# Gathering the hidden rows of 64 dense tokens during the routing, and plain float32 operands for the U blocks done ahead

## The chip, the cores and the metric

The kernel runs on one core of one Trainium2 chip. Its engines are TensorE (PE, with its weight loads as PEld), VectorE (DVE), ScalarE (ACT), GpSimd (POOL) and SyncE (SP), which here only issues transfers. The metric is the device time of one execution in microseconds, as the median of the runs.

## The reference, cut to what matters

One encoder layer for 512 tokens of width 1024: two attentions, a layer norm, and then

```
h = LN2(alpha * h + PEER(h) + sigmoid(h @ W_g + b_g) * (p @ W_ple))
```

PEER is a feed-forward layer with 16384 single-neuron experts, row e of U and of V being expert e. For each token and each of 8 heads, the query's two halves are scored against 128 sub-keys each, the 16 best of each half are combined, and the 16 best sums give 16 experts e = 128 * e1 + e2 with softmax weights g. So 128 experts for a token:

```
PEER(h)[t] = sum over its 128 experts e of  g[t, e] * gelu(U[e] . h[t]) * V[e]
```

## The kernel before, in words

The attentions and the first layer norm leave h (four tiles of 128 tokens, h[0] to h[3]) and its transpose in two parts, hTh and hTl, in a reduced float32 format (fp32r), whose sum is h. A product of two such pairs is three matmuls (mm3, L89 to L92: high by high, high by low, low by high); split (L72) makes the parts, a cast on ScalarE (L75) and a subtraction on VectorE (L76). stream (L81) loads a block as raw and splits it into whi and wlo.

PEER is computed in two ways. The first 128 tokens (chunk 0, N_G) are *gathered*: for each of their 128 experts k, gather_u (L861) fetches one row of U per token by an indirect transfer that POOL issues (128 rows of 4 KB into a gat buffer, of which there are four), and VectorE forms the 128 dot products with h (L865). After all 128, one Gelu and one multiplication by the weights; then gather_v does the same with V and adds into base (L876). That is 257 steps. The other 384 tokens (chunks 1 to 3, N_D) are *dense*: all 16384 experts are computed in 128 blocks of 128. expert_in (L616) loads a U block, splits it, and makes its hidden values for all 384 tokens, 24 matmuls of 128x384 into hp, then Gelu (L623) into ge. expert_out (L886) multiplies the activations a = ge * G, split into a_hi and a_lo, by the V block, 18 matmuls of 128x512 into six acc tiles that stay in PSUM. G holds the weights of all tokens for all experts, zero where an expert isn't chosen.

G is made in the routing. route (L691) finds for a chunk the expert numbers (as e1 and e2) and weights gw, on VectorE; for chunk 0 it ends in i_sel (L760), the list for the gathers. build_g (L764) turns e1, e2 and gw of a dense chunk into rows of G: per token a one-hot matrix by e1 and a weighted one by e2 (L779 to L788), one plain float32 matmul (L793), a copy on ScalarE (L796), and a store (L797) to g_dram. Since this leaves TensorE idle, a generator filler (L803) yields other work: the output gate (8 steps with its products, L821 to L824), and the first LEAD = 40 U blocks, of which the first SPILL = 16 go to ge_dram and the others stay in ge buffers. run_fill takes 1.6 filler steps per step of route and 0.9 per step of build_g. The chunks are routed in the order 1, 2, 3, 0. In this part a scheduler orders each engine's instructions.

The main loop (L905 to L947) goes over the 128 blocks. VectorE's order is as written there. Each step n does expert_in(n + 40) while there is one, loads every eighth step a gt tile with G for eight blocks (load_g, L897 to L902), loads the V block as v_raw (L914) and splits it, multiplies ge by gt (L932), splits the result, does expert_out, and then as many gather steps as are due: 257 / (128 - 0.75 * LEAD - 3) for a step with an expert_in, a quarter of that for one without. The pools of the routing (pR: rt, rg) are closed ahead of it, and pE, with gt, gat, v_raw, v_hi, v_lo, a_hi and a_lo, takes their memory. whi, wlo and raw come from wst, which stays.

At the end (L958) acc is added to base, and the last layer norm and the stores follow.

Of the kernel before, what the change touches and what calls it, by code (L numbers as in the profile page):

```python
# [9 lines left out]
F32 = mybir.dt.float32  # L10
F32R = mybir.dt.float32r
I32 = mybir.dt.int32
# [7 lines left out]
T = 512  # L20
# [7 lines left out]
QD = 96  # L28
N_G = 128
N_D = T - N_G  # L30
GT = 16
GB = 8
LEAD = 40
SPILL = 16
FILL_ROUTE = 1.6
FILL_G = 0.9
OT = 8
OV = 5
NEG = -1e30
# [12 lines left out]
def tile_encoder_layer(ctx: ExitStack, tc: tile.TileContext, A: dict, out: bass.AP):  # L52
# [16 lines left out]
    def r32(ap):  # L69
        return ap.bitcast(F32)  # L70
# [10 lines left out]
    def stream(src, shape, scale=None):  # L81
        raw = wst.tile([128] + shape, F32, name="raw", bufs=3)
        nc.sync.dma_start(raw, src)
        hi = wst.tile([128] + shape, F32R, name="whi")
        lo = wst.tile([128] + shape, F32R, name="wlo")
        split(hi, lo, raw, scale)
        return hi, lo
# [514 lines left out]

    NGC, NDC = N_G // 128, N_D // 128
    NTG = N_D // GT
    ts = slice(N_G, T)
    u_rows, v_rows = A["u_rows"], A["v_rows"]
    ge_dram = dram.tile([SPILL, 128, N_D], F32, name="ge_dram")
    g_dram = dram.tile([NTG, 128, 128 * GT], F32, name="g_dram")

    pB = ctx.enter_context(tc.tile_pool(name="pB", bufs=1))  # L610
# [2 lines left out]
    i_sel = pB.tile([128, NGC, 128], I32, name="i_sel")  # L613
    ge_t = {}

    def expert_in(i):  # L616

        u = stream(A["uT"][i], [8, 128])
        ps = psH.tile([128, 512], F32, name="hp")
        for k in range(8):  # L620
            mm3(ps[:, :N_D], (u[0][:, k], u[1][:, k]), (hTh[:, k, ts], hTl[:, k, ts]), k == 0, k == 7)
        ge = pB.tile([128, N_D], F32, name="ge", bufs=LEAD - SPILL + 2)
        nc.scalar.activation(ge, ps[:, :N_D], AF.Gelu)  # L623
        if i < SPILL:
            nc.sync.dma_start(ge_dram[i], ge)
        else:
            ge_t[i] = ge
# [63 lines left out]
    def route(c, res):  # L691

        v = v_all[:, c]
        ixf = rt.tile([128, 8, 2, 16], F32, name="tk_if")
        nc.vector.tensor_copy(ixf, i_all[:, c])
        cand = rt.tile([128, 8, N_CAND], F32, name="cand")

        def v1(a, na, n):
            return v[:, :, 0, a:a + na].unsqueeze(3).to_broadcast([128, 8, na, n])

        def v2(na, n):
            return v[:, :, 1, 0:n].unsqueeze(2).to_broadcast([128, 8, na, n])

        a = 0
        while a < 16:
            na = sum(1 for x in ROW_N if x == ROW_N[a])
            n = ROW_N[a]
            o = cand[:, :, ROW_ST[a]:ROW_ST[a] + na * n].rearrange("p h (a n) -> p h a n", n=n)
            nc.vector.tensor_tensor(o, v1(a, na, n), v2(na, n), op=OP.add)
            a += na  # L710
        cv = rt.tile([128, 8, 16], F32, name="cv")
        ci = rt.tile([128, 8, 16], U32, name="ci")
        for hd in range(8):
            tmp = rt.tile([128, N_CAND], F32, name="tk_t2", bufs=2)
            top16(cv[:, hd], ci[:, hd], cand[:, hd, :], tmp)
        yield
        cif = rt.tile([128, 8, 16], F32, name="cif")
        nc.vector.tensor_copy(cif, ci)
        gw = g_sel[:, c, :] if c < NGC else rt.tile([128, 128], F32, name="gw")
        g3 = gw.rearrange("p (h k) -> p h k", k=16)  # L720
        nc.vector.tensor_tensor(g3, cv, cv[:, :, 0:1].to_broadcast([128, 8, 16]), op=OP.subtract)
        nc.scalar.activation(gw, gw, AF.Exp)
        wt = rt.tile([128, 8, 16], F32, name="wt")
        nc.vector.tensor_copy(wt[:, :, 0:1], ixf[:, :, 0, 0:1])
        nc.vector.tensor_tensor(wt[:, :, 1:16], ixf[:, :, 0, 1:16], ixf[:, :, 0, 0:15], op=OP.subtract)
        nc.vector.scalar_tensor_tensor(wt, wt, 64.0, dst_c.unsqueeze(1).to_broadcast([128, 8, 16]),
                                       op0=OP.mult, op1=OP.add)
        big = rt.tile([128, 8, 16, 16], F32, name="big")
        b3 = big.rearrange("p h k a -> p (h k) a")
        cf = cif.rearrange("p h k -> p (h k)")  # L730
        nc.vector.tensor_tensor(b3, cf.unsqueeze(2).to_broadcast([128, 128, 16]),
                                start_c.unsqueeze(1).to_broadcast([128, 128, 16]), op=OP.is_ge)
        yield
        gs = rt.tile([128, 8], F32, name="gs")
        nc.vector.reduce_sum(gs, g3, axis=AX.X)
        nc.vector.reciprocal(gs, gs)
        nc.vector.tensor_tensor(g3, g3, gs.unsqueeze(2).to_broadcast([128, 8, 16]), op=OP.mult)
        nc.vector.tensor_tensor(big, big, wt.unsqueeze(2).to_broadcast([128, 8, 16, 16]), op=OP.mult)
        es = rt.tile([128, 128], F32, name="es")
        nc.vector.reduce_sum(es, b3, axis=AX.X)  # L740
        ei = rt.tile([128, 128], I32, name="ei")
        nc.vector.tensor_copy(ei, es)
        sti = rt.tile([128, 128], I32, name="sti")
        nc.vector.tensor_scalar(sti, ei, 63, None, op0=OP.bitwise_and)
        nc.vector.tensor_scalar(ei, ei, 6, None, op0=OP.arith_shift_right)
        e1 = rt.tile([128, 128], F32, name="e1")
        nc.vector.tensor_copy(e1, ei)
        bb = rt.tile([128, 128], F32, name="bb")
        nc.vector.tensor_copy(bb, sti)
        nc.vector.tensor_tensor(bb, cf, bb, op=OP.subtract)  # L750
        yield
        big = rt.tile([128, 8, 16, 16], F32, name="big")
        b3 = big.rearrange("p h k a -> p (h k) a")
        nc.vector.tensor_tensor(b3, bb.unsqueeze(2).to_broadcast([128, 128, 16]),
                                iota[:, 0:16].unsqueeze(1).to_broadcast([128, 128, 16]), op=OP.is_equal)
        nc.vector.tensor_tensor(big, big, ixf[:, :, 1, :].unsqueeze(2).to_broadcast([128, 8, 16, 16]), op=OP.mult)
        e2 = rt.tile([128, 128], F32, name="e2")
        nc.vector.reduce_sum(e2, b3, axis=AX.X)
        if c < NGC:
            nc.vector.scalar_tensor_tensor(i_sel[:, c, :], e1, 128.0, e2, op0=OP.mult, op1=OP.add)  # L760
        res.extend((e1, e2, gw))
        yield
# [35 lines left out]
            yield  # L798


    gb = row_bcast(rg, A["gate_b"], "gb")

    def filler():  # L803
        blocks = iter(range(LEAD))
        for hf in range(2):
            hs = slice(hf * 512, (hf + 1) * 512)
            gps = [ps_tile("mm", 4) for _ in range(4)]
            for kk in range(4):
                w = stream(A["gate_w"][kk * 256:(kk + 1) * 256, hs].rearrange("(k p) n -> p k n", p=128), [2, 512])
                for k2 in range(2):  # L810
                    k = 2 * kk + k2
                    for c in range(4):
                        cs = slice(c * 128, (c + 1) * 128)
                        mm3(gps[c], (hTh[:, k, cs], hTl[:, k, cs]), (w[0][:, k2], w[1][:, k2]), k == 0, k == 7)
                yield

            for c in range(4):
                pl = rg.tile([128, 512], F32, name="pl", bufs=2)
                nc.sync.dma_start(pl, ple_dram[c, :, hs])
                z = rg.tile([128, 512], F32, name="z", bufs=2)  # L820
                nc.vector.tensor_tensor(z, gps[c], gb[:, hs], op=OP.add)  # L821
                nc.scalar.activation(z, z, AF.Tanh, scale=0.5)
                nc.vector.scalar_tensor_tensor(z, z, 1.0, pl, op0=OP.add, op1=OP.mult)
                nc.vector.scalar_tensor_tensor(base[c][:, hs], h[c][:, hs], ALPHA, z, op0=OP.mult, op1=OP.add)  # L824
                if c % 2:
                    expert_in(next(blocks))
                    yield
        for i in blocks:
            expert_in(i)
            yield  # L830

    fill = filler()
# [7 lines left out]
            due -= 1  # L840

    run_fill(0)
    for c in list(range(NGC, 4)) + list(range(NGC)):
        res = []
        for _ in route(c, res):
            run_fill(FILL_ROUTE)
        if c >= NGC:
            for _ in build_g(c, *res):
                run_fill(FILL_G)
    for _ in fill:  # L850
        pass
    pR.close()
# [52 lines left out]
    with tc.manual_schedule(engines={nc.vector.engine}):  # L905
        for n, i in enumerate(order):
# [17 lines left out]
                al = pE.tile([128, N_D], F32R, name="a_lo")  # L924
            split(vh, vl, raw)
            if i < SPILL:
                ge = pE.tile([128, N_D], F32, name="ge_in", bufs=2)
                nc.sync.dma_start(ge, ge_dram[i])
            else:
                ge = ge_t.pop(i)  # L930
            g3 = ge.rearrange("p (g t) -> p g t", t=GT)
            nc.vector.tensor_tensor(g3, g3, gt[:, :, n % GB, :], op=OP.mult)  # L932
            split(ah, al, ge)
            late.append((n, ah, al, vh, vl))
            if n < 124:
                for c in range(NDC):
# [112 lines left out]
```

## Time and profile before

| | |
|---|---|
| time, median of 3 runs (lowest to highest) | 1650.75 us (1648.87 to 1651.54) |
| the profiled execution's own time | 1650.28 us |
| its span | 1648.4 us |
| granted TensorE clock, mean | 0.994 |
| q1, transfers issued by SP and others | 234.52 MB, 41.3% of 16 engines' span |
| q0, indirect transfers issued by POOL | 140.00 MB, 24.2% |
| read from HBM, written | 339.61 MB, 32.51 MB |
| landing of a U block, a V block, a gt tile (median) | 6.2, 6.7, 15.0 us |
| landing of a gather from U, from V (median) | 7.9, 6.9 us |

The span is the time from the first instruction to the last in the trace of that execution; 1.88 us of its time lie outside. By line, a group's row reads: line, engine, operation, tile written <- tiles read, shape, count, then busy us and mean ns of one, then the engine's idle time just ahead of such instructions with what ended it. A row of the timeline reads: start us, duration us, the same names, and in brackets the idle time ahead of it. Matmuls are pipelined, so a pace is read from start to start. All helpers' instructions carry the helper's line (L75, L76, L90 to L92), so they are told apart by their tiles. A plain float32 matmul shows as two records. Busy time is a mean over stages; three stages matter here: the routing with the blocks ahead (about 427 to 742 us), the main loop with U blocks (to about 1470 us), and the rest of the main loop.

### The profile page before, as it was taken

Reading aid. Unit: us, or ns where it says so; the run is one execution under the profiler, and the core shown is the slowest. Engines: PE = TensorE matmul, PEld = TensorE weight load, DVE = VectorE, ACT = ScalarE, POOL = GpSimd, SP = SyncE. Lnnn points to the kernel's source line nnn. Section 1 sums busy time; section 2 is a strip of 40 time slices with the busy share of each in tenths; the row PEclk is TensorE's granted clock in tenths of the full one; section 3 lists DMA queues with packets and bytes.
Section 4 is the critical chain, followed back from the end, with each engine's and each line's share of the span. In section 5 each row is a group of like instructions: output and inputs, shape, how many; then the busy total and the mean of one; then the engine's idle time right before and its main releaser. Section 6 shows DMA issues by size and latency. Waiting matters only on the chain.

```text
span 1648.4 us, 24146 instructions
## 1 busy us (share of the span) xinstructions
PE 1599.4 (97%) x8547; PEld 1414.1 (86%) x8547; DVE 1318.0 (80%) x2873; ACT 729.9 (44%) x1233; POOL 391.6 (24%) x335
## 2 busy tenths in 40 slices
PE   6999899999999999999999999999999999999997
PEld 4788677888789999999999999999999999988886
DVE  7366794599999999958888787877888888877776
ACT  3356683433357485853333333333333333333343
POOL 1013100000000000005544443443444444432200
PEclk9999999999999999999999999999999999999999
DMA  7242330332336554579989989899899899977773
GB/s 222 62 126 73 87 122 14 120 88 82 116 140 226 174 210 154 192 281 333 350 301 342 319 318 332 307 343 319 299 335 323 314 335 319 329 250 260 247 244 115
DMA packets 180888, 376.05 MB, mean 228 GB/s; under 512 B 13216, under 2 KB 99616, under 8 KB 177696
## 3 DMA queue, kind: packets, MB, share of 16 engines
q1 hardware_dynamic: 141216, 234.52, 41.3%
q0 software_dynamic: 39552, 140.00, 24.2%
q8 instruction: 67, 1.10, 0.3%
q14 instruction: 53, 0.43, 0.1%
HBM read 339.61 MB, written 32.51 MB: 226 GB/s over the span
## 4 chain that ended last, share of the span: by engine, by line
PE 85%; DVE 10%; ACT 1%; DMA 1%; issue 1%; SPq 0%; ACTq 0%; DVEq 0%
PE acc L92 10%; PE acc L90 10%; PE acc L91 10%; PE hp L92 10%; PE hp L90 10%; PE hp L91 10%; PE mm L90 3%; PE pj L90 3%; PE pj L91 3%; PE pj L92 3%; PE mm L91 3%; PE mm L92 3%; PE tr L793 3%; DVE oh_j L788 2%; DVE wlo L76 1%; PE tr L191 1%
## 5 line engine op out<-in xcount | busy, mean ns | idle before, releaser
L92 PE MATMUL hp<-hTh,wlo 128*128 128x384 f32 x1024 | 347.8, 340 | 5.5 <-DVE wlo L76 5.5
L90 PE MATMUL hp<-hTh,whi 128*128 128x384 f32 x1024 | 347.8, 340 | 1.9 <-ACT ge L623 1.9
L91 PE MATMUL hp<-hTl,whi 128*128 128x384 f32 x1024 | 346.8, 339 | 0.0
L863 POOL DMA_INDIRECT gat<-in_u_rows_dram,i_sel x128 | 175.4, 1370 | 622.1 <-issue 424.2
L92 PE MATMUL acc<-v_hi,a_lo 128*128 128x512 f32 x756 | 294.9, 390 | 0.0
L91 PE MATMUL acc<-v_lo,a_hi 128*128 128x512 f32 x756 | 294.7, 390 | 0.0
L90 PE MATMUL acc<-v_hi,a_hi 128*128 128x512 f32 x756 | 294.5, 390 | 0.0
L75 ACT CAST whi<-raw 128x1024 fp32r<-128x1024 f32 (+3 forms) x181 | 184.6, 1020 | 225.8 <-PE hp L91 115.7
L76 DVE TENSOR_TENSOR wlo<-raw,whi 128x1024 fp32r<-128x1024 f32 (+3 forms) x181 | 213.0, 1179 | 58.0 <-ACT whi L75 57.4
L75 ACT CAST v_hi<-v_raw 128x1024 fp32r<-128x1024 f32 x126 | 132.9, 1055 | 268.3 <-issue 226.7
L874 POOL DMA_INDIRECT gat<-in_v_rows_dram,i_sel x128 | 178.1, 1392 | 261.3 <-DVE base L876 230.7
L76 DVE TENSOR_TENSOR v_lo<-v_raw,v_hi 128x1024 fp32r<-128x1024 f32 x126 | 154.1, 1223 | 70.8 <-ACT v_hi L75 70.8
L92 PEld LDWEIGHTS hp<-hTh,wlo 128*128 128x128 f32 x1024 | 193.8, 189 | 8.0 <-DVE wlo L76 7.9
L90 PEld LDWEIGHTS hp<-hTh,whi 128*128 128x128 f32 x1024 | 193.9, 189 | 5.7 <-ACT ge L623 2.2
L91 PEld LDWEIGHTS hp<-hTl,whi 128*128 128x128 f32 x1024 | 193.8, 189 | 3.4
L876 DVE SCALAR_TENSOR_TENSOR base<-gat,hdot,base 128x1024 f32<-128x1024 f32 x128 | 164.1, 1282 | 15.3 <-DMA gat<-in_v_rows_dram,i_sel 13.3
L865 DVE SCALAR_TENSOR_TENSOR scr<-gat,h 128x1024 f32<-128x1024 f32 x128 | 156.5, 1223 | 15.6 <-DMA gat<-in_u_rows_dram,i_sel 13.4
L92 PEld LDWEIGHTS acc<-v_hi,a_lo 128*128 128x128 f32 x756 | 141.9, 188 | 30.7 <-DVE a_lo L76 1.2
L90 PEld LDWEIGHTS acc<-v_hi,a_hi 128*128 128x128 f32 x756 | 142.0, 188 | 27.1 <-ACT a_hi L75 0.7
L91 PEld LDWEIGHTS acc<-v_lo,a_hi 128*128 128x128 f32 x756 | 141.9, 188 | 26.4
L75 ACT CAST a_hi<-ge 128x384 fp32r<-128x384 f32 x112 | 57.5, 513 | 217.7 <-DVE ge L932 217.7
L76 DVE TENSOR_TENSOR a_lo<-ge,a_hi 128x384 fp32r<-128x384 f32 x112 | 62.6, 559 | 70.9 <-ACT a_hi L75 70.9
(321 smaller groups left out, 2454.1 us busy)
## 6 DMA issues: line engine op xcount, KB each, us to landing
raw<-in_uT_dram SPq DMA_DIRECT2D x128, 512.0 KB, 6.2
v_raw<-in_v_rows_dram SPq DMA_DIRECT2D x128, 512.0 KB, 6.7
g_dram<-g_st SPq DMA_DIRECT2D x24, 1024.0 KB, 4.3
gt<-g_dram SPq DMA_DIRECT2D x16, 1536.0 KB, 15.0
raw<-in_w_in_dram SPq DMA_DIRECT2D x17, 512.0 KB, 3.8
raw<-in_w_q_dram SPq DMA_DIRECT2D x16, 512.0 KB, 3.9
na_b<-in_na_bias_dram POOLq DMA_DIRECT2D x32, 128.0 KB, 2.4
raw<-in_w_o_dram SPq DMA_DIRECT2D x8, 512.0 KB, 3.7
```

The costliest lines, as they stand in the source:

```text
L75: nc.scalar.copy(hi, src)
L76: nc.vector.tensor_tensor(lo, src, r32(hi), op=OP.subtract)
L90: nc.tensor.matmul(ps, a[0], b[0], start=start, stop=False)
L91: nc.tensor.matmul(ps, a[0], b[1], start=False, stop=False)
L92: nc.tensor.matmul(ps, a[1], b[0], start=False, stop=stop)
L191: nc.tensor.transpose(ps[:, i * 128:(i + 1) * 128], p[:, i * 128:(i + 1) * 128], ident)
L788: nc.vector.tensor_scalar(oj[:, i], iota, eT[:, 1, t0 + i:t0 + i + 1], eT[:, 2, t0 + i:t0 + i + 1], op0=OP.is_equal, op1=OP.mult)
L793: nc.tensor.matmul(ps[:, i * 128:(i + 1) * 128], oj[:, 4 * r + i, :], oi[:, 4 * r + i, :], start=True, stop=True)
L863: nc.gpsimd.indirect_dma_start(out=u[:], out_offset=None, in_=u_rows, in_offset=bass.IndirectOffsetOnAxis(ap=i_sel[:, c, k:k + 1], axis=0))
L865: nc.vector.scalar_tensor_tensor(scr, u, 1.0, h[c], op0=OP.mult, op1=OP.mult, accum_out=hdot[:, c, k:k + 1])
L874: nc.gpsimd.indirect_dma_start(out=u[:], out_offset=None, in_=v_rows, in_offset=bass.IndirectOffsetOnAxis(ap=i_sel[:, c, k:k + 1], axis=0))
L876: nc.vector.scalar_tensor_tensor(base[c], u, hdot[:, c, k:k + 1], base[c], op0=OP.mult, op1=OP.add)
```

## The change

Chunk 1's first 64 tokens (N_S) get their hidden values by gathering during the routing: own_rows forms their list of experts, spreads it by two small transfers over all 128 partitions (64 tokens by two halves of 64 experts), and does 64 indirect gathers of 128 rows of U into the whi and wlo slots, with a dot on VectorE each. After Gelu, two transfers bring the values back, and gw is multiplied by them, so that these tokens enter G with output instead of weight. The U blocks then cover 320 tokens (N_U), in the routing and in the main loop; the multiplication with gt is done in place in gt, on 320 of its 384 columns, and the split reads gt. The order becomes route 1, route and build 2, route and build 3, the gathers that are left, build 1, route 0; own_rows is drawn with 2.8 steps per step of route or build.

The blocks ahead, now 44, are multiplied in plain float32: the raw U tile by `whole`, the sum of hTh and hTl that POOL makes once (8 additions, in the pool rg of the routing), 8 matmuls of 128x320 a block without a split. The gate's sum z is formed in PSUM in place of a tile. The filler's rates go to 1.7 and 1.0.

```
+N_S = 64
+N_U = N_D - N_S
-LEAD = 40
+LEAD = 44
-FILL_ROUTE = 1.6
-FILL_G = 0.9
+FILL_ROUTE = 1.7
+FILL_G = 1.0
+FILL_S = 2.8
...
-    def expert_in(i):
-        u = stream(A["uT"][i], [8, 128])
+    def expert_in(i, whole=None):
         ps = psH.tile([128, 512], F32, name="hp")
+        if whole is None:
+            u = stream(A["uT"][i], [8, 128])
+            for k in range(8):
+                mm3(ps[:, :N_U], (u[0][:, k], u[1][:, k]), (hTh[:, k, ts], hTl[:, k, ts]), k == 0, k == 7)
+        else:
+            u = wst.tile([128, 8, 128], F32, name="raw", bufs=3)
+            nc.sync.dma_start(u, A["uT"][i])
+            for k in range(8):
+                nc.tensor.matmul(ps[:, :N_U], u[:, k], whole[:, k, :], start=(k == 0), stop=(k == 7))
...
+    h_s = rg.tile([128, D], F32, name="h_s")
+    for j in range(PARTS):
+        nc.sync.dma_start(h_s[j * N_S:(j + 1) * N_S, :], h[NGC][0:N_S, :])
+    whole = rg.tile([128, 8, N_U], F32, name="whole")
+    for k in range(8):
+        nc.gpsimd.tensor_tensor(whole[:, k, :], r32(hTh[:, k, ts]), r32(hTl[:, k, ts]), op=OP.add)
+    def own_rows(e1, e2, gw):
+        ix = rg.tile([N_S, 128], I32, name="s_ix")
+        nc.vector.scalar_tensor_tensor(ix, e1[0:N_S], 128.0, e2[0:N_S], op0=OP.mult, op1=OP.add)
+        sel = rg.tile([128, SLOTS], I32, name="s_sel")
+        for j in range(PARTS):
+            nc.sync.dma_start(sel[j * N_S:(j + 1) * N_S, :], ix[:, j * SLOTS:(j + 1) * SLOTS])
+        dots = rg.tile([128, SLOTS], F32, name="s_dot")
+        for k in range(SLOTS):
+            u = wst.tile([128, D], F32, name=("whi", "wlo")[k % 2])
+            nc.gpsimd.indirect_dma_start(out=u[:], out_offset=None, in_=u_rows,
+                                         in_offset=bass.IndirectOffsetOnAxis(ap=sel[:, k:k + 1], axis=0))
+            nc.vector.scalar_tensor_tensor(u, u, 1.0, h_s, op0=OP.mult, op1=OP.mult, accum_out=dots[:, k:k + 1])
+            yield
+        nc.scalar.activation(dots, dots, AF.Gelu)
+        act = rg.tile([N_S, 128], F32, name="s_ix")
+        for j in range(PARTS):
+            nc.sync.dma_start(act[:, j * SLOTS:(j + 1) * SLOTS], dots[j * N_S:(j + 1) * N_S, :])
+        nc.vector.tensor_tensor(gw[0:N_S], gw[0:N_S], act, op=OP.mult)
...
-                z = rg.tile([128, 512], F32, name="z", bufs=2)
-                nc.vector.tensor_tensor(z, gps[c], gb[:, hs], op=OP.add)
+                z = gps[c]
+                nc.vector.tensor_tensor(z, z, gb[:, hs], op=OP.add)
...
-            g3 = ge.rearrange("p (g t) -> p g t", t=GT)
-            nc.vector.tensor_tensor(g3, g3, gt[:, :, n % GB, :], op=OP.mult)
-            split(ah, al, ge)
+            a = gt[:, :, n % GB, :]
+            dn = gt[:, N_S // GT:, n % GB, :]
+            nc.vector.tensor_tensor(dn, dn, ge.rearrange("p (g t) -> p g t", t=GT), op=OP.mult)
+            split(ah.rearrange("p (g t) -> p g t", t=GT), al.rearrange("p (g t) -> p g t", t=GT), a)
```

More of the change, by code (lines that the diff above doesn't have):

```diff
@@ L604, in tile_encoder_layer @@
     NTG = N_D // GT
-    ts = slice(N_G, T)
+    ts = slice(T - N_U, T)
     u_rows, v_rows = A["u_rows"], A["v_rows"]
-    ge_dram = dram.tile([SPILL, 128, N_D], F32, name="ge_dram")
+    ge_dram = dram.tile([SPILL, 128, N_U], F32, name="ge_dram")
     g_dram = dram.tile([NTG, 128, 128 * GT], F32, name="g_dram")
@@ L614, in tile_encoder_layer @@
     ge_t = {}
-    def expert_in(i):
-        u = stream(A["uT"][i], [8, 128])
+    def expert_in(i, whole=None):
         ps = psH.tile([128, 512], F32, name="hp")
[L620 to L623, printed above, removed]
+        if whole is None:
[7 more added lines that the diff above has]
+                nc.tensor.matmul(ps[:, :N_U], u[:, k], whole[:, k, :], start=(k == 0), stop=(k == 7))
+        ge = pB.tile([128, N_U], F32, name="ge", bufs=LEAD - SPILL + 2)
+        nc.scalar.activation(ge, ps[:, :N_U], AF.Gelu)
         if i < SPILL:
@@ L718, in route @@
         nc.vector.tensor_copy(cif, ci)
-        gw = g_sel[:, c, :] if c < NGC else rt.tile([128, 128], F32, name="gw")
+        own = "s" if c == NGC else ""
+        gw = g_sel[:, c, :] if c < NGC else rt.tile([128, 128], F32, name="gw" + own)
         g3 = gw.rearrange("p (h k) -> p h k", k=16)
@@ L745, in route @@
         nc.vector.tensor_scalar(ei, ei, 6, None, op0=OP.arith_shift_right)
-        e1 = rt.tile([128, 128], F32, name="e1")
+        e1 = rt.tile([128, 128], F32, name="e1" + own)
         nc.vector.tensor_copy(e1, ei)
@@ L756, in route @@
         nc.vector.tensor_tensor(big, big, ixf[:, :, 1, :].unsqueeze(2).to_broadcast([128, 8, 16, 16]), op=OP.mult)
-        e2 = rt.tile([128, 128], F32, name="e2")
+        e2 = rt.tile([128, 128], F32, name="e2" + own)
         nc.vector.reduce_sum(e2, b3, axis=AX.X)
@@ L798, in build_g @@
             yield
+    PARTS, SLOTS = 128 // N_S, 128 * N_S // 128
+    h_s = rg.tile([128, D], F32, name="h_s")
[22 more added lines that the diff above has]
+        nc.vector.tensor_tensor(gw[0:N_S], gw[0:N_S], act, op=OP.mult)
     gb = row_bcast(rg, A["gate_b"], "gb")
@@ L825, in filler @@
                 if c % 2:
-                    expert_in(next(blocks))
+                    expert_in(next(blocks), whole)
                     yield
         for i in blocks:
-            expert_in(i)
+            expert_in(i, whole)
             yield
@@ L842, in tile_encoder_layer, with run_own @@
     run_fill(0)
-    for c in list(range(NGC, 4)) + list(range(NGC)):
+    gathers, g_due = iter(()), 0.0
+    def run_own(amount):
+        nonlocal g_due
+        g_due += amount
+        while g_due >= 1:
+            next(gathers, None)
+            g_due -= 1
+    held = []
+    for c in list(range(NGC, 4)):
         res = []
@@ L846, in tile_encoder_layer @@
             run_fill(FILL_ROUTE)
-        if c >= NGC:
-            for _ in build_g(c, *res):
-                run_fill(FILL_G)
+            run_own(FILL_S)
+        if c == NGC:
+            held = res
+            gathers = own_rows(*res)
+            continue
+        for _ in build_g(c, *res):
+            run_fill(FILL_G)
+            run_own(FILL_S)
+    for _ in gathers:
+        pass
+    for _ in build_g(NGC, *held):
+        run_fill(FILL_G)
+    for c in range(NGC):
+        for _ in route(c, []):
+            run_fill(FILL_ROUTE)
     for _ in fill:
@@ L926, in tile_encoder_layer @@
             if i < SPILL:
-                ge = pE.tile([128, N_D], F32, name="ge_in", bufs=2)
+                ge = pE.tile([128, N_U], F32, name="ge_in", bufs=2)
                 nc.sync.dma_start(ge, ge_dram[i])
```

## The prediction

> **What bounds the kernel now.** I read the page's totals first, then the busy time by stretch, then the instruction groups, then single rows of each engine.
>
> ```profile
> span 1648.4 us, 24146 instructions
> PE 1599.4 (97%) x8547; PEld 1414.1 (86%) x8547; DVE 1318.0 (80%) x2873; ACT 729.9 (44%) x1233; POOL 391.6 (24%) x335
> ```
> TensorE is busy for 97% of the span, but that is a mean over stages. By stretch (columns: PE, PEld, DVE, ACT and POOL busy us, granted clock, DMA share, GB/s):
> ```profile
> 427.00:717.00 290.00, 277.84 (x1753) 261.68 (x1752) 288.75 (x876) 187.16 (x385) 0.00 (x0) 0.99 0.49 178
> 800.00:1400.00 600.00, 600.00 (x3054) 547.86 (x3053) 485.23 (x597) 218.18 (x293) 263.26 (x196) 1.00 0.92 324
> 805.00:825.00 20.00, 20.00 (x105) 18.53 (x104) 15.87 (x22) 7.07 (x9) 9.90 (x8) 1.00 1.04 368
> ```
> In the routing (427 to 717) VectorE works 288.75 of 290 us and so sets the pace, and TensorE is filled to 96% by the blocks done ahead; DMA is half idle and POOL idle. In the main loop (800 to 1400) TensorE is busy without a gap, VectorE 81%, and the DMA engines move 324 GB/s; in a busy 20 us they moved 368 at a share of 1.04, so some 365 GB/s is all that they have shown. The routing ends with i_sel; the main loop starts with the first acc:
> ```profile
> 717.42 0.29 DVE L760 SCALAR_TENSOR_TENSOR i_sel<-e,e 128x128 int32<-128x128 f32 x1
> 741.95 0.53 PE L92 MATMUL hp<-hTh,wlo 128*128 128x384 f32 x1 [0.25 <-DVE wlo L76]
> 751.60 0.39 PE L90 MATMUL acc<-v_hi,a_hi 128*128 128x512 f32 x1
> ```
> One iteration, from its acc to the next one's:
> ```profile
> 900.16 0.39 PE L90 MATMUL acc<-v_hi,a_hi 128*128 128x512 f32 x1
> ...
> 904.25 0.34 PE L90 MATMUL hp<-hTh,whi 128*128 128x384 f32 x1
> ...
> 908.41 0.39 PE L90 MATMUL acc<-v_hi,a_hi 128*128 128x512 f32 x1
> ```
> 18 acc matmuls take 4.09 us and 24 hp matmuls 4.16 us (173 ns each): 8.25 us. After 751.60 there come 86 such iterations and 42 that have an acc alone: 86 x 8.25 + 42 x 4.09 = 881.3; the span's other 15.5 us (1648.4 - 751.6 - 881.3) are small stalls and the layer norm at the end. I keep that residue.
>
> **The change, part by part.**
>
> *Main loop, TensorE.* The U matmuls get 320 columns instead of 384. The trace has none of 320, but has 256:
> ```profile
> 317.74 0.28 PE L92 MATMUL mm<-hTh,wlo 128*128 128x256 f32 x1
> ...
> 322.33 0.28 PE L92 MATMUL mm<-hTh,wlo 128*128 128x256 f32 x1
> ```
> 39 starts lie between these: 118 ns for 256 columns. Halfway to 173 is 145.5 ns, so a block takes 24 x 0.1455 = 3.49 us and an iteration 7.58 on TensorE, 0.67 less. LEAD 44 takes four blocks more out of the loop.
>
> *Main loop, VectorE.* Is it fast enough for 7.58? A 3-dot iteration of before, from wlo to wlo, where no gather is late, and one dot that is late:
> ```profile
> 773.89 1.22 DVE L76 TENSOR_TENSOR wlo<-raw,whi 128x1024 fp32r<-128x1024 f32 x1
> 775.03 1.22 DVE L76 TENSOR_TENSOR v_lo<-v_raw,v_hi 128x1024 fp32r<-128x1024 f32 x1
> 776.16 0.55 DVE L932 TENSOR_TENSOR ge<-ge,gt 128x384 f32<-128x384 f32 x1
> 777.35 0.56 DVE L76 TENSOR_TENSOR a_lo<-ge,a_hi 128x384 fp32r<-128x384 f32 x1 [0.63 <-ACT a_hi L75]
> ...
> 779.08 1.22 DVE L865 SCALAR_TENSOR_TENSOR scr<-gat,h 128x1024 f32<-128x1024 f32 x1
> ...
> 780.35 1.23 DVE L865 SCALAR_TENSOR_TENSOR scr<-gat,h 128x1024 f32<-128x1024 f32 x1
> ...
> 781.50 1.22 DVE L76 TENSOR_TENSOR wlo<-raw,whi 128x1024 fp32r<-128x1024 f32 x1
> ...
> 788.63 1.23 DVE L865 SCALAR_TENSOR_TENSOR scr<-gat,h 128x1024 f32<-128x1024 f32 x1 [0.70 <-DMA gat<-in_u_rows_dram,i_sel]
> ```
> 7.61 us with three dots (1.27 apart). The 257 gather steps spread over 128 - 33 - 3 = 92 units instead of 95: 2.79 a block instead of 2.71. So 7.61 - 0.21 x 1.27 - 0.09 (the g multiplication with 320 columns, a sixth of 0.55) = 7.25 us, with nothing late. The one late gather shown costs 0.70; with one in two or three iterations late, 7.5 to 7.6. VectorE thus reaches 7.6 just where TensorE does.
>
> *Main loop, DMA.*
> ```profile
> raw<-in_uT_dram SPq DMA_DIRECT2D x128, 512.0 KB, 6.2
> ...
> gt<-g_dram SPq DMA_DIRECT2D x16, 1536.0 KB, 15.0
> ```
> Per iteration a U block and a V block (0.524 MB each), 2.79 gathers of 128 rows of 4 KB (0.524 MB), and an eighth of gt (1536 KB): 2.71 MB; at 7.58 us that is 357 GB/s, against 324 now and the 368 shown at best. At 350 it takes 7.74 us. Three engines with 7.58, 7.25 plus waits and about 7.4 to 7.75 don't mesh without loss: I take **7.75** us, bounds 7.58 (TensorE alone) and 8.25 (as now).
>
> The Trainium skill speaks against this part: "DMA: Bandwidth & Descriptors", section Specifications, gives about 358 GB/s as one core's share of the memory. By it an iteration could not be under 2.71 MB / 358 = 7.57 us, and would leave nothing for lateness; the trace's 368 over 20 us lies 3% above that figure, so it is no hard ceiling here.
>
> *Routing, VectorE (the bound there).* Blocks ahead lose the split, the 64 tokens bring dots:
> ```profile
> L76 DVE TENSOR_TENSOR wlo<-raw,whi 128x1024 fp32r<-128x1024 f32 (+3 forms) x181 | 213.0, 1179 | 58.0 <-ACT whi L75 57.4
> L865 DVE SCALAR_TENSOR_TENSOR scr<-gat,h 128x1024 f32<-128x1024 f32 x128 | 156.5, 1223 | 15.6 <-DMA gat<-in_u_rows_dram,i_sel 13.4
> L863 POOL DMA_INDIRECT gat<-in_u_rows_dram,i_sel x128 | 175.4, 1370 | 622.1 <-issue 424.2
> ```
> A wlo occupies 1.14 us back to back (773.89 to 775.03), a dot 1.27. Of the 40 blocks six ran after i_sel (717 to 742 is 24 us, 4.16 each), so 34 splits go: -39 us; 64 dots come: +81. That is +42 (if all 40 counted, +36). The index and weight operations (lines 823 and 838 of the changed kernel) are about 1 us; z in place is the same count. i_sel then falls at about **760**. The gathers' issues (64 x 1.37 = 88 us) lie on POOL, idle in this stretch, as do the eight additions for `whole`. SP issues five small transfers besides. Their bytes, 64 x 0.524 = 33.5 MB in some 300 us, are 110 GB/s on top of 178: cover is ample. If the four slots (whi, wlo, two each) made every dot wait, one dot per quarter of a round trip (1.27 + 1.37 + a landing of 8, over 4 = 2.7 us) instead of 1.27 would be up to +90; but the routing has 876 VectorE instructions (the 427 to 717 row), which the scheduler can put between the dots, so I take at most +5 on the 760 and keep more for a rival.
>
> *Routing, TensorE.* Plain float32 takes 8 matmuls a block, each as two records:
> ```profile
> 599.89 1.95 PE L793 MATMUL tr<-oh_i,oh_j 128*128 128x128 f32 x16
> 601.60 0.42 PE L90 MATMUL hp<-hTh,whi 128*128 128x384 f32 x1
> L793 PE MATMUL tr<-oh_i,oh_j 128*128 128x128 f32 x768 | 99.7, 280 | 4.0 <-DVE oh_j L788 4.0
> ```
> 16 records of 128 columns in 1.71 us: 107 ns each, and 768 records for 384 matmuls. By columns, 320 take 267 ns, a block 16 x 0.267 = 4.28 us (ends: 16 x 0.1455 = 2.3 at the fp32r pace, 16 x 0.280 = 4.5 with the mean record). 44 x 4.28 - 40 x 4.16 = **+22** us on TensorE; its blocks ahead ended just before 741.95, so not before 763. By the VectorE reading i_sel is at 760 to 765 and the last few blocks follow. I take the end of block 43 at **769**.
>
> *The transition.* Today gt, V blocks and gathers are loaded while TensorE still has 24 us of blocks ahead (717 to 742):
> ```profile
> L900 SPq DMA_DIRECT2D gt<-g_dram x16: 370/378/992, 721.1 to 1566.5; - x16
> DMA to landing us min/median/max: 9.5/15.0/18.1
> ```
> In the changed program the first gt load, the V loads and the first gathers go to memory that `whole` held, and `whole` is read by the last plain matmul; so they wait for the end of block 43. Behind the waiting gt load SP queues the V loads, POOL the gathers, VectorE v_lo and the first dots. TensorE then has one split block (3.5 us) and starts of two more. gt lands after 9.5 to 18.1 us, taken as 13, then the multiplication and the split (2 us): first acc at 769 + 15 = **784**, +32.4 against 751.6. Cost of the wait: some 8 us, since without it acc could begin at about 776.
>
> *Sum.* After the first acc come 83 U blocks and 45 acc alone: 784 + 83 x 7.75 + 45 x 4.09 + 15.5 = 1626.8 us of span. The profiled execution took 1650.28 us (1.88 outside its span), 0.5 under the median of 1650.75: 1629 in the terms of the median. Break-even is 8.01 us an iteration.
>
> **The rivals.**
>
> (a) *TensorE alone decides.* Gathers stay ahead, as VectorE's idle 19% now suggests, and an iteration takes 7.58: 784 + 629.1 + 184.1 + 15.5 = 1612.7, time 1615; with the transition hidden as well, 1607. Against it: 357 GB/s sustained has been seen for 20 us only. Chance 0.2.
>
> (b) *Forecast*: 7.65 to 7.95 an iteration, time 1621 to 1646, likeliest 1629. Chance 0.52.
>
> (c) *Slower: the gather round trip keeps the iteration.* Four gat buffers, each held for issue, landing and dot:
> ```profile
> gat<-in_u_rows_dram,i_sel POOLq DMA_INDIRECT x128, 7.9
> ```
> 1.37 + 7.9 + 1.27 = 10.5 us, over four buffers 2.6 a gather, times 2.79 = 7.35 an iteration: under 7.6 now, but the landing grows where the DMA engines are full, and at 8.9 us it takes 8.05, beyond the break-even of 8.01. With the iteration back at 8.25 the span is 784 + 684.8 + 184.1 + 15.5 = 1668.4, time 1671; nothing pays for the +32 ahead. For it: VectorE did wait on gathers. Against: over 128 dots that wait was 13.4 us in all (the L865 row). Chance 0.16.
>
> (d) *The dots are not hidden in the routing*: the 64 gathers stall VectorE (slots, landing) by 10 to 20 us more, and a 7.75 loop follows: 1639 to 1649, about no change. Chance 0.12.
>
> **How the numbers follow.** The likeliest case gives 1629. For the range I leave out the far end of (c) and the lowest of (a): 1607 to 1658. Faster by more than 0.2% (3.3 us, about what a measurement of this kernel can tell) means under 1647.4: all of (a) and (b) and half of (d), 0.76. Within 0.2%, 1647.4 to 1654: part of (d) and the near end of (c), 0.08. Slower: 0.16.
>
> **What would show it.** Right: i_sel at 755 to 770, the first acc 10 to 16 us after the last plain matmul with TensorE idle in between, plain records near 267 ns apart, fp32r 320 records near 145 ns, iterations of 7.6 to 7.9 with gaps on TensorE that are released by VectorE's a_lo, wlo or by v_raw, DMA near 350 GB/s. Wrong: TensorE without gaps at 7.58 (then a); DMA share over 1.0 with gather landings of 9 us and more and iterations over 8 (then c); VectorE idle behind gathers between 430 and 720 (then d); plain blocks of 2.3 us would move the end of the routing to VectorE alone.

## The result, and the profile after

The changed kernel takes **1643.8 us** (median of 12 runs, 1638.09 to 1648.35), the kernel before 1650.68 (12 runs): the ratio is 0.9957, 95% interval 0.9943 to 0.9971. It is 0.4% faster, clear of the interval, but by 7 us where 22 were forecast. The profiled execution's span is 1642.7 us, 15.9 more than the 1626.8 of the sum.

First the page of the changed kernel, then its stages (columns as before: PE, PEld, DVE, ACT and POOL busy us, granted clock, DMA share, GB/s):
```profile
span 1642.7 us, 23609 instructions
PE 1564.1 (95%) x8195; PEld 1309.7 (80%) x8195; DVE 1328.0 (81%) x2959; ACT 671.3 (41%) x1190; POOL 553.3 (34%) x407
```
```profile
427.00:717.00 290.00, 279.69 (x1416) 216.56 (x1415) 282.81 (x829) 137.83 (x311) 101.38 (x72) 1.00 0.78 282
747.00:800.00 53.00, 37.00 (x167) 29.60 (x166) 29.75 (x39) 12.23 (x18) 12.37 (x10) 0.84 0.78 276
800.00:1400.00 600.00, 583.93 (x3152) 520.27 (x3151) 498.36 (x633) 206.60 (x301) 338.17 (x209) 0.99 0.95 338
```
The routing is about as full as it was on VectorE (282.81 busy us of 290, before 288.75) and TensorE, and the gathers went into DMA time that was free (178 to 282 GB/s). Two things are new: a hole on TensorE between 747 and 800 us, and, in a main loop where TensorE had no gap, 16 us without work in 600.

The end of the routing in the changed kernel, VectorE, then SyncE's issues of transfers, then TensorE (the last row is from the end of the U blocks):
```profile
758.77 0.29 DVE L771 SCALAR_TENSOR_TENSOR i_sel<-e,e 128x128 int32<-128x128 f32 x1
...
779.76 1.23 DVE L79 TENSOR_TENSOR v_lo<-v_raw,v_hi 128x1024 fp32r<-128x1024 f32 x1 [19.56 <-DMA v_raw<-in_v_rows_dram]
780.90 0.49 DVE L995 TENSOR_TENSOR gt<-gt,ge 128x320 f32<-128x320 f32 x1
```
```profile
762.48 0.38 SPq L962 DMA_DIRECT2D gt<-g_dram  x1
762.91 9.91 SPq L976 DMA_DIRECT2D v_raw<-in_v_rows_dram  x3
```
```profile
752.83 9.58 PE L631 MATMUL hp<-whole,raw 128*128 128x320 f32 x35
762.00 0.55 PE L93 MATMUL hp<-hTh,whi 128*128 128x320 f32 x1
...
781.99 0.79 PE L93 MATMUL acc<-v_hi,a_hi 128*128 128x512 f32 x1 [14.17 <-ACT a_hi L78]
...
1447.17 0.40 PE L93 MATMUL acc<-v_hi,a_hi 128*128 128x512 f32 x1
```
i_sel comes at 758.77, the last plain record just before 762, the first acc at 781.99 after 14.17 us of idle TensorE. 35 plain records take 9.17 us, 262 ns each. The row at 1447.17 is the start of the 84th acc: (1447.17 - 781.99) / 83 = **8.01 us** an iteration. 50 of the 83 take 7.64 to 7.66 us, which is TensorE's own pace now (the fp32r matmul of 320 columns measures 147 ns from start to start); the others are longer, up to 12.03.

Who makes them longer? The waits of VectorE and TensorE in the changed kernel, 800 to 1400 us (total us, times, longest):
```profile
DVE scr L927 <- DMA gat<-in_u_rows_dram,i_sel: 32.5, 30, 3.2
DVE base L938 <- DMA gat<-in_v_rows_dram,i_sel: 17.3, 21, 2.0
```
```profile
PE hp L95 <- DVE wlo L79: 15.7, 19, 2.8
```
And the same of the kernel before, where TensorE had no wait in this stretch at all:
```profile
DVE base L876 <- DMA gat<-in_v_rows_dram,i_sel: 11.8, 11, 1.7
DVE scr L865 <- DMA gat<-in_u_rows_dram,i_sel: 11.2, 17, 1.3
```
VectorE waits twice as long for gathered rows, and now TensorE waits behind it, for the low half of the next U block. One such case in full, the POOL and the VectorE timeline of the changed kernel:
```profile
1105.91 1.81 POOL L925 DMA_INDIRECT gat<-in_u_rows_dram,i_sel  x1 [3.33 <-DVE scr L927]
1108.02 1.27 POOL L925 DMA_INDIRECT gat<-in_u_rows_dram,i_sel  x1 [0.30 <-issue]
```
```profile
1104.41 1.22 DVE L927 SCALAR_TENSOR_TENSOR scr<-gat,h 128x1024 f32<-128x1024 f32 x1
...
1105.67 1.23 DVE L927 SCALAR_TENSOR_TENSOR scr<-gat,h 128x1024 f32<-128x1024 f32 x1
...
1114.98 1.22 DVE L927 SCALAR_TENSOR_TENSOR scr<-gat,h 128x1024 f32<-128x1024 f32 x1 [1.49 <-DMA gat<-in_u_rows_dram,i_sel]
...
1117.54 1.22 DVE L927 SCALAR_TENSOR_TENSOR scr<-gat,h 128x1024 f32<-128x1024 f32 x1 [1.32 <-DMA gat<-in_u_rows_dram,i_sel]
```
With four buffers, gather k + 4 is issued when dot k is done. The dot of 1104.41 frees its buffer at 1105.63, the issue runs from 1105.91 to 1107.72, and the dot that reads it starts at 1114.98, 7.3 us later and 1.49 us late; the one after it likewise. Pairing all issues and dots of the U phase in order (128 each), a dot that waited starts 7.0 us after the end of its issue (median of 32 dots); before the change it was 6.8 (20 dots). An issue takes 1.59 us on the mean, before 1.37.

### The profile page after: what moved, and what is told of

The parts are those of the page before. It is cut to its first block, busy times and chain, and to the rows that moved or that the text cites. A ratio compares the mean times of both kernels' runs of the same rounds, so it can differ in the third digit from the quotient of the medians.

```text
span 1642.7 us, 23609 instructions
## 1 busy us (share of the span) xinstructions
PE 1564.1 (95%) x8195; PEld 1309.7 (80%) x8195; DVE 1328.0 (81%) x2959; ACT 671.3 (41%) x1190; POOL 553.3 (34%) x407
## 4 chain that ended last, share of the span: by engine, by line
PE 40%; DMA 22%; issue 15%; DVE 14%; POOL 7%; ACT 2%; SPq 1%; DVEq 0%; POOLq 0%; ACTq 0%
DMA gat<-in_u_rows_dram,i_sel 11%; DMA gat<-in_v_rows_dram,i_sel 8%; PE hp L631 4%; PE acc L93 4%; PE acc L95 4%; PE acc L94 4%; POOL gat L925 3%; PE tr L804 3%; PE pj L93 3%; PE mm L93 3%; PE pj L94 3%; PE pj L95 3%; PE mm L94 3%; PE mm L95 3%; POOL gat L936 3%
## 5 line engine op out<-in xcount | busy, mean ns | idle before, releaser
L78 ACT CAST a_hi<-gt 128x384 fp32r<-128x384 f32 x126 | 64.9, 515 | 478.7 <-DVE gt L995 476.5
L95 PE MATMUL hp<-hTh,wlo 128*128 128x320 f32 x672 | 211.2, 314 | 17.9 <-DVE wlo L79 17.5
L93 PE MATMUL hp<-hTh,whi 128*128 128x320 f32 x672 | 208.7, 311 | 1.0 <-ACT ge L633 1.0
L94 PE MATMUL hp<-hTl,whi 128*128 128x320 f32 x672 | 208.2, 310 | 0.0
L631 PE MATMUL hp<-whole,raw 128*128 128x320 f32 x704 | 200.3, 433 | 0.0
L78 ACT CAST whi<-raw 128x1024 fp32r<-128x1024 f32 (+3 forms) x137 | 138.4, 1010 | 131.2 <-PE mm L94 53.1
L79 DVE TENSOR_TENSOR wlo<-raw,whi 128x1024 fp32r<-128x1024 f32 (+3 forms) x137 | 159.8, 1167 | 37.7 <-ACT whi L78 37.3
L631 PEld LDWEIGHTS hp<-whole,raw 128*128 128x128 f32 x704 | 128.9, 190 | 45.6
L95 PEld LDWEIGHTS hp<-hTh,wlo 128*128 128x128 f32 x672 | 127.3, 189 | 26.0 <-DVE wlo L79 25.9
L79 DVE TENSOR_TENSOR a_lo<-gt,a_hi 128x384 fp32r<-128x384 f32 x126 | 70.4, 559 | 80.4 <-ACT a_hi L78 79.1
```

Of the source, the lines that this page charges most:

```text
L78: nc.scalar.copy(hi, src)
L79: nc.vector.tensor_tensor(lo, src, r32(hi), op=OP.subtract)
L93: nc.tensor.matmul(ps, a[0], b[0], start=start, stop=False)
L94: nc.tensor.matmul(ps, a[0], b[1], start=False, stop=False)
L95: nc.tensor.matmul(ps, a[1], b[0], start=False, stop=stop)
L631: nc.tensor.matmul(ps[:, :N_U], u[:, k], whole[:, k, :], start=(k == 0), stop=(k == 7))
```

## The experiments

**Theory A.** The round trip of a gather through its buffer, from the end of one dot to the start of the dot four later, is 0.3 (until the issue starts) + 1.6 (issue) + 7.0 (landing, from the issue's end) = 8.9 us. An iteration's two or three dots stand together at its end. In two iterations of three dots each, the second and third dot read buffers that were freed just one iteration before, so their round trip has 7.65 us. Before, TensorE's 8.25 us left VectorE 0.6 us an iteration (its own three-dot iteration is 7.61) in which a late dot could be made up. **Theory B.** The transfers: 2.71 MB in 8.01 us (338 GB/s) is what the DMA engines deliver. **Theory C.** VectorE's own work and order take the time. Beside these, the runs look at the transition at 760 us and at what each half of the change does alone.

*More buffers.*
```
-        u = pE.tile([128, D], F32, name="gat", bufs=4)
+        u = pE.tile([128, D], F32, name="gat", bufs=5)
```


> The changed kernel with five gat buffers in the main loop instead of four. Theory A (the round trip of a gather through its buffer holds VectorE back: issue about 1.6 us, landing about 7.0, against 7.65 us between the end of a dot and the start of the fourth dot after it): most stalls go, the mean iteration falls from 8.01 to 7.7 or 7.8, time 1618 to 1628. Theory B (the bytes: 2.71 MB in 8.01 us are what the DMA engines deliver): no change, 1638 to 1648.

Measured 1619.11 us (ratio to before 0.9811, 0.9793 to 0.9829): 25 us from one buffer of 4 KB a partition. The stretch 800 to 1400 of this kernel, and VectorE's waits in it:
```profile
800.00:1400.00 600.00, 599.89 (x3297) 540.83 (x3297) 526.72 (x662) 225.23 (x317) 356.44 (x222) 1.00 0.98 357
```
```profile
DVE scr L927 <- DMA gat<-in_u_rows_dram,i_sel: 7.5, 6, 2.6
...
DVE base L938 <- DMA gat<-in_v_rows_dram,i_sel: 1.8, 2, 1.6
```
VectorE's waits for rows fall from 49.8 to 9.3 us, TensorE is busy again without a gap, the mean iteration is 7.67, and the DMA engines deliver 357 GB/s for 600 us. So 338 GB/s was not all that they could deliver: Theory B is out.

*Six buffers.* The dot's product goes back into its buffer instead of scr, which makes room.
```
-        nc.vector.scalar_tensor_tensor(scr, u, 1.0, h[c], op0=OP.mult, ...
+        nc.vector.scalar_tensor_tensor(u, u, 1.0, h[c], op0=OP.mult, ...
```


> Six gat buffers; to make room the dot's product is written back into its gat buffer and the tile scr is left out. Theory A: nearly all stalls behind gathers go, mean iteration 7.65 to 7.70, time 1614 to 1622, and DMA share above 0.97 in the main loop. Theory B: no change, 1638 to 1648.

Measured 1619.19 (0.9815, 0.9795 to 0.9836), mean iteration 7.67: five were enough.

*Three buffers.*
```
-        u = pE.tile([128, D], F32, name="gat", bufs=4)
+        u = pE.tile([128, D], F32, name="gat", bufs=3)
```

> The changed kernel with three gat buffers. Theory A: a buffer's round (issue 1.6, gap 0.3, landing 7.0, dot 1.27) of 10.2 us over three buffers gives a gather per 3.4 us, 2.79 of them 9.5 us an iteration: time 1642 + 83 x 1.5 = 1767, between 1735 and 1790. If the landing falls because the DMA engines are less full, the lower end.

Measured 1740.8 (1.0561, 1.0519 to 1.0603), mean iteration 9.11 for the 9.5 reckoned: at the lower end. Here a late dot starts 6.4 us after the end of its issue (7.0 with four buffers), and the DMA engines move 297 GB/s. The time moves as the theory says on both sides of four buffers.

*The same four buffers, another order.* One due dot goes behind the split of U and one behind the split of V; gathers, bytes and buffers are unchanged.
```
             if n + LEAD < 128:
                 expert_in(n + LEAD)
+            if n >= 2 and len(due_now) > 1:
+                due_now.pop(0)()
...
             split(vh, vl, raw)
+            if n >= 2 and len(due_now) > 1:
+                due_now.pop(0)()
```


> The changed kernel, four gat buffers, same gathers and bytes; only VectorE's order differs: of an iteration's two or three dots one stands behind the split of U and one behind the split of V, instead of all at the iteration's end. Theory A in its full form (in a burst the second and third dot find a buffer that was freed 7.65 us before, against 8.9 for issue and landing; evenly spread there are 4 x 2.74 - 1.27 = 9.7 us): most stalls go, iteration 7.65 to 7.75, time 1614 to 1624. If only the number of buffers matters and not the burst, no change: 1638 to 1648.

Measured 1619.66 (0.9823, 0.9802 to 0.9845), iteration 7.70; VectorE's waits in 800 to 1400:
```profile
DVE scr L927 <- DMA gat<-in_u_rows_dram,i_sel: 11.2, 17, 1.8
...
DVE base L938 <- DMA gat<-in_v_rows_dram,i_sel: 2.5, 5, 1.1
```
So it is not the number of buffers by itself but the burst on four of them. An issue also takes 1.45 us here instead of 1.59, but that alone would leave a round trip of 8.8 us, still over 7.65. This order gives the 24 us back for no memory.

*Fewer bytes, same gathers.* A V block is loaded in every second step and used twice.
```
-            raw = pE.tile([128, D], F32, name="v_raw", bufs=3)
-            nc.sync.dma_start(raw, v_rows[i * 128:(i + 1) * 128, :])
+            if n % 2 == 0:
+                raw = pE.tile([128, D], F32, name="v_raw", bufs=3)
+                nc.sync.dma_start(raw, v_rows[i * 128:(i + 1) * 128, :])
```


> The changed kernel, but a V block is loaded only in every second step and used in both (the output is not the layer's: half of V is left out). Bytes of an iteration fall from 2.71 to 2.45 MB, four gat buffers as before. Theory B: the stalls go, iteration about 7.65, time 1612 to 1622. Theory A: issue and landing stay, so most stalls stay: landing perhaps 0.5 us shorter, iteration 7.85 to 8.0, time 1629 to 1643.

Measured 1635.71 (0.9913, 0.989 to 0.9937), iteration 7.89. VectorE's waits for rows are still there, at 311 GB/s:
```profile
DVE scr L927 <- DMA gat<-in_u_rows_dram,i_sel: 25.6, 24, 2.3
DVE base L938 <- DMA gat<-in_v_rows_dram,i_sel: 14.4, 18, 1.6
```
The load of the DMA engines has a share in the lateness (8 us of 25), not the main one.

*No gathers in the main loop.* The 256 operations of chunk 0 read tiles that are in place (h[1] for the rows of U, scr for those of V).
```
-        u = pE.tile([128, D], F32, name="gat", bufs=4)
-        nc.gpsimd.indirect_dma_start(out=u[:], out_offset=None, in_=u_rows, ...
+        u = h[NGC]
```

> The changed kernel without the gathers of the main loop: the 256 dots and accumulations of chunk 0 read tiles that are in place (the gathered rows of chunk 0 are left out, VectorE's work stays). Both theories: VectorE has 7.25 us of work an iteration and TensorE 7.65, so no stalls, iteration 7.65, time 1612 to 1616; if iterations over 7.8 stay, the stalls are VectorE's own order and both theories fall.

Measured 1610.97 (0.976, 0.9743 to 0.9778), 1 us under the range; mean iteration 7.67, first acc at 778.31. VectorE's order needs no more time than TensorE: theory C is out. This is the floor of the main loop: five buffers are 8 us above it, of which 7.4 stand ahead of the first acc (785.68 against 778.31).

*Five buffers in the kernel before* (with the dot written back into its buffer).

> The kernel before with five gat buffers (room made by writing the dot's product back into the buffer, without scr). Control of theory A: before the change VectorE's late gathers cost no TensorE time (88 iterations of 8.25 us without a gap), so the fifth buffer gives nothing: 1647 to 1652. If it gains over 3 us, four buffers were already a cost and the change did not make it.

Measured 1652.23 (1.0012, 1.0001 to 1.0024), every iteration 8.25. The fourth buffer's shortage cost nothing until TensorE's iteration got shorter.

*The 64 tokens alone*: the blocks ahead keep their split operands.
```
-                    expert_in(next(blocks), whole)
+                    expert_in(next(blocks))
...
-            expert_in(i, whole)
+            expert_in(i)
```


> The changed kernel with split operands for the 44 blocks ahead (the 64 tokens' gathering alone). VectorE gets 44 x 1.14 = 50 us more in the routing, TensorE 44 x 0.73 = 32 us less: the routing is VectorE's alone, i_sel at about 805, first acc at about 825 to 830, main loop as in the changed kernel: 1683 to 1695. If i_sel stays near 760, VectorE was not the bound of the routing.

Measured 1757.12 (1.0636, 1.0609 to 1.0663), first acc at 899.66: some 70 us slower than expected. The gathers of the routing on POOL, and the two longest of what POOL waited for ahead of them (total us, times):
```profile
L830 POOL DMA_INDIRECT whi<-in_u_rows_dram,s_sel x32: 939/954/2753, 481.1 to 787.9; - x32
...
  PE hp L95: 85.2, 12
  DVE oh_j L799: 65.6, 15
```
The gathers use the slots of whi and wlo, which the splits now need too. A gather can then wait for a block's matmuls, and the next block's split for a dot. The next run takes that away.

*The 64 tokens alone, with buffers of their own.*
```
-            u = wst.tile([128, D], F32, name=("whi", "wlo")[k % 2])
+            u = rg.tile([128, D], F32, name="s_u", bufs=4)
```


> As the run with split operands for the blocks ahead, but the 64 gathers of the routing have four buffers of their own instead of the slots of whi and wlo (24 blocks spilled to make room, whole left out). If the 118 us that the first acc came later there were 50 us of VectorE work and the rest the sharing of the slots by splits and gathers: first acc at 825 to 840, time 1685 to 1700. If VectorE's waits stay for another reason, first acc stays beyond 870 and the time over 1730.

Measured 1687.33 (1.0238, 1.0202 to 1.0272), first acc at 828.16, both in the range. i_sel comes at 810.0, 51 us later than in the changed kernel, for the 50 us of VectorE's splits that were reckoned. The other 70 us of the run before went with the sharing of the slots. Plain operands for the blocks ahead thus do two things for the gathering: they free VectorE, and they leave the slots empty.

*The plain operands alone*: the kernel before with 40 plain blocks of 384 columns.
```
-                    expert_in(next(blocks))
+                    expert_in(next(blocks), whole)
...
-            expert_in(i)
+            expert_in(i, whole)
```

> The kernel before with plain float32 operands for its 40 blocks ahead (384 columns) and z in PSUM, without the 64 tokens. VectorE loses 46 us in the routing, but a plain block of 384 columns takes 16 x 0.32 = 5.1 us against 4.16: TensorE gets 38 us more and becomes the bound; i_sel at 680 to 710, first acc at 775 to 785, main loop as before (8.25): 1672 to 1684. If the time stays within 3 us of before, the plain blocks are hidden.

Measured 1688.85 (1.0232, 1.0214 to 1.025), 5 us above the range, with the first acc at 791.51 for 775 to 785: TensorE idles 11.7 us ahead of it, which the expectation had left out. So the plain operands alone cost 2.3%, and the 64 tokens alone 2.4% with buffers of their own and 6.4% in the slots; together the two halves are 0.4% faster.

*Covering the transition*: five buffers, 48 blocks ahead of which the last four are split, and other gather weights.
```
-LEAD = 44
-SPILL = 16
+LEAD = 48
+SPILL = 24
...
-            expert_in(i, whole)
+            expert_in(i, whole if i < 44 else None)
...
-            spent += 1 if n + LEAD < 128 else 0.25
+            spent += 1 if n + LEAD < 128 else 0.35
```


> The changed kernel with five gat buffers, and 48 blocks ahead, of which the last four use split operands and so do not read whole; 24 blocks spilled; a step without a U block takes 0.35 gather steps instead of 0.25. The transition theory (TensorE idles 14 to 16 us ahead of the first acc because gt and v_raw start only when the routing's last reader is done): four blocks of 3.55 us cover it, idle under 4 us, first acc still at 783 to 790, 79 iterations of 7.65 to 7.7, time 1604 to 1609. Rival: the four extra loads and splits push v_raw and the first acc back by as much, time 1615 to 1621.

Measured 1611.25 (0.9761, 0.9742 to 0.9779), above the 1604 to 1609 expected and under the rival's range. The first acc comes at 789.24 and all 79 iterations take 7.65, as expected. TensorE's idle time ahead of the first acc is 6.4 us, where the run with five buffers has 16.4 and under 4 was expected. The 49 steps without a U block take 4.27 us from start to start instead of 4.12, which gives 7 us back.

The same with the old gather weights:
```
-            spent += 1 if n + LEAD < 128 else 0.35
+            spent += 1 if n + LEAD < 128 else 0.25
```


> The run with 48 blocks ahead and five gat buffers, with 0.25 gather steps a step without a U block instead of 0.35. There the last 49 steps took 4.26 us instead of 4.11, from VectorE's and the transfers' work in them; now 2.89 gathers stand in each U iteration, 2.76 MB, 361 GB/s at 7.65 us. If that rate is delivered: 79 x 7.65 and 49 x 4.11, time 1604 to 1608. If the DMA engines stop at the 357 GB/s seen so far: iterations of 7.73, time 1609 to 1614.

Measured **1608.37** (0.9764, 0.9733 to 0.9796), the best version here. Its main loop:
```profile
800.00:1400.00 600.00, 600.00 (x3294) 540.75 (x3293) 531.18 (x664) 223.56 (x313) 368.07 (x228) 1.00 0.99 361
```
361 GB/s are delivered and the iterations stay at 7.65; the last 49 steps take 4.15, where 4.11 was expected, and the time is just above the 1604 to 1608 of that case. It doesn't stand clear of the run before it within the intervals.

## Why the prediction was wrong, point by point

- *Routing.* Right. i_sel was put at 760 and came at 758.77; plain records at 267 ns, measured 262; the last plain block at 769, measured 762. The runs of the halves bear out the balance: with split blocks VectorE's end of the routing moves out by 51 us, and with plain blocks of 384 columns the first acc moves out by 40.
- *Transition.* Right that gt and the V blocks start late: both are issued behind the last plain matmul, at 762.48 and 762.91. The first acc, 784 and measured 781.99, is near by luck, since two errors cancel: it came 20 us after the last plain block instead of 15, and that block ended 7 us earlier. What it waited for was v_raw, queued on SP behind gt, and not gt, which was there at 780.90.
- *Main loop, TensorE.* 7.58, measured 7.65: the interpolation between 256 and 384 columns gave 145.5 ns a matmul for (7.65 - 4.09) / 24 = 148.
- *Main loop, the mean iteration.* **This is the step that failed**: 7.75 was taken, 8.01 measured, 83 x 0.264 = +21.9 us, more than the whole miss of 15.9 (first acc -2.0, everything behind the 84th acc -4.0). The term that was too small is VectorE's waiting for gathers, "7.25 plus waits", put at 7.5 to 7.6. In 800 to 1400 us it waits 49.8 us in about 75 iterations, 0.66 each, so about 7.9 before any other wait, and TensorE waits behind it. By the run without gathers (7.67), 0.34 of the 8.01 comes from the gathers. A ceiling of the DMA engines, which the prediction weighed most, is not among the causes; their load has a share, 8 us of 25.
- *The residue of 15.5 us* was miscounted. The kernel before has 87 iterations with a U block after its first acc and 41 steps without, not 86 and 42: the last of those 87 ends at 1469.64, and 751.60 + 87 x 8.25 = 1469.35. That leaves some 11.4 us and not 15.5, and the changed kernel has 11.5. This is the -4.0, and it hid part of the miss.
- *The rival (c)* named the right mechanism, the round trip through four buffers, and played it down by a mean: 2.6 us a gather times 2.79 is 7.35, under 7.6. Its 10.5 us also counts the issue twice, since the landing of 7.9 us in that row runs from the issue's start. Counted once, with the changed kernel's numbers, it is 0.3 + 1.6 + 7.0 + 1.27 = 10.2 us, over four buffers 7.1 an iteration: the mean says even less of a shortage. But the dots come in bursts, and a dot has to be on time one by one. Its condition, a landing that grows from 7.9 to 8.9 us, was not needed: for late dots, the time from the issue's start to the dot is 8.3 us (median), before 8.1. The round trip grew from 8.5 to 8.9 us, and the time that it has shrank from 8.25 to 7.65.
- *The late gather* shown in the prediction (0.70 us) was priced at one in two or three iterations. That fits the kernel before (28 waits of 0.82 us in some 73 iterations), where it cost TensorE nothing. In the changed kernel there are 51 waits of 0.98 us in some 75.
- *The Trainium skill's* figure, "DMA: Bandwidth & Descriptors", section Specifications, about 358 GB/s a core: 357 over 600 us agrees, and 361 in the last run is 1% above it. No run here was held up by it.

## What to carry to other kernels

When the bound engine's iteration is cut, take the round trip of each buffer that the second engine waits for, and compare it with the time between the freeing of a buffer and its next use, operation by operation: a mean rate hides a burst. An idle share of 19% on an engine doesn't say that its waits are free; ask what they cost once the slack that pays for them is gone. Spreading the consumers was here as good as another buffer, and needed none.

## What the runs showed of the hardware

*A gap on TensorE can cost more than itself.* After the gap of 2.35 us at 1119.96 in the changed kernel:
```profile
1119.96 0.41 PE L95 MATMUL hp<-hTh,wlo 128*128 128x320 f32 x1 [2.35 <-DVE wlo L79]
1120.21 0.31 PE L93 MATMUL hp<-hTh,whi 128*128 128x320 f32 x1
1120.36 0.31 PE L94 MATMUL hp<-hTl,whi 128*128 128x320 f32 x1
...
1121.15 0.47 PE L95 MATMUL hp<-hTh,wlo 128*128 128x320 f32 x1
1121.42 0.47 PE L93 MATMUL hp<-hTh,whi 128*128 128x320 f32 x1
...
1124.24 0.31 PE L95 MATMUL hp<-hTh,wlo 128*128 128x320 f32 x1
```
The starts are 147 ns apart, then for 3 us 267 ns, then 147 again. The 22 matmuls from 1119.96 to the next acc at 1124.83 take 4.87 us where 22 x 0.147 is 3.23: 1.6 us more, and the granted clock of 1120 to 1124 us is 0.58. The gap of 2.81 us at 807.19 cost 1.4 us more in the same way, while gaps of 1.13 to 1.41 us in this kernel lost under 0.2. The Trainium skill, "TensorE: Matmul & The Clock Gate", section "Part 1: The HAM clock gate (the "warmup" mystery)", puts the half clock behind at least one idle window of about 3.4 us; here gaps of 2.81 and 2.35 us were enough. The length of the gap alone doesn't decide it: in the run with three buffers, one of 2.35 us was followed by the full pace, at a granted clock of 1.00 in 1222 to 1226 us:
```profile
1222.34 0.41 PE L95 MATMUL hp<-hTh,wlo 128*128 128x320 f32 x1 [2.35 <-DVE wlo L79]
...
1223.91 0.31 PE L93 MATMUL hp<-hTh,whi 128*128 128x320 f32 x1
1224.06 0.31 PE L94 MATMUL hp<-hTl,whi 128*128 128x320 f32 x1
```
What else decides it stays open. Over the 83 U iterations of the changed kernel, the gaps add up to 17.5 us of the 30 by which they exceed 7.65; the slow pace after these two gaps makes 3, and that after the hole ahead of the first acc 2.

*A gather's issue waits for VectorE.* With VectorE idle (763.26 to 767.95 in the changed kernel, four issues), POOL's issue took 0.94 us; begun during an operation of VectorE, up to 1.98. The issue at 1105.91 above ran 1.81 us beside the dot of 1105.67 that ends at 1106.90: 0.82 us are left after that, not far from an undisturbed issue. Of the main loop's 256 issues in the changed kernel 29 began with VectorE idle and took 0.94 to 0.95 us; the other 227 ended 0.82 us after the operation in which they began (median). The Trainium skill, "SBUF — State Buffer", section "Who interferes with whom", has VectorE operations with two inputs in SBUF contend with GpSimd's reads, and these rows agree with that. The same section says that `tensor_tensor` did not stall DMA in a probe; here the 101 issues begun during v_lo and wlo, which are such operations, show the same 0.82 us. No run here took the contention away by itself.
